# Group C's projections read the latents in row order through a strided moving operand

## The chip, the cores and the metric

The kernel runs on one core of a Trainium2 chip. The core has five engines that run side by side and wait for each other by semaphores: TensorE (PE, matmuls; its weight loads are a row of their own, PEld), VectorE (DVE), ScalarE (ACT), GpSimd (POOL) and SyncE (SP, which issues most transfers). The metric is the time of one execution in microseconds, the median of several runs. Beside the times there is one profiled execution, with every instruction's start and duration.

## The reference

Two layers of a mixer over 512 latent tokens (a grid of 8 rows by 64 columns) and 256 context tokens. Each layer normalises and modulates its input, projects it once, runs three groups of attention heads on parts of the projection, multiplies their outputs by a SiLU gate, projects back and adds. Group A is global attention, group B a neighbourhood on the grid, group C a sliding window over the tokens in row order. Only what concerns the change is shown.

```
def layer(x, cx, ..., need_ctx):
    hx = rmsnorm(x, norm_w) * (1 + scale[:, None, :]) + shift[:, None, :]
    hc = rmsnorm(cx, norm_w) * (1 + scale_c) + shift_c
    px = split_cols(hx @ w_in)
    pc = split_cols(hc @ w_in)
    ...
    yc_, ycc = window_gqa(px[6], px[7], px[8], pc[6], pc[7], pc[8], cos, sin, sink, need_ctx)
    ux = jnp.concatenate([ya, yb, yc_], axis=-1) * jax.nn.silu(px[9])
    x = x + gate[:, None, :] * (ux @ w_out)

def window_gqa(q, k, v, qc, kc, vc, cos, sin, sink, need_ctx):
    """+-WINDOW sliding-window GQA with per-head sink logit, banded 128-query blocks."""
    q = (apply_rope(heads(q, N_HEADS_C), cos, sin) * scale).reshape(B, N, N_KV_C, G, HEAD_DIM)
    k = apply_rope(heads(k, N_KV_C), cos, sin)
    ...
```

## The kernel before

**Layout.** The latents lie in SBUF with the model dimension on partitions, eight tiles of 128, and the tokens along the free dimension. The tokens stand in column order: position 8 * column + row, so that group B's window on the grid is a contiguous stretch of keys. Each tile exists twice, as a rounded high part (`hh`) and the remainder (`hl`), in the matmul type fp32r; weights are split in the same way (`wh`, `wl`). A product is the sum of three matmuls, high by high, high by low, low by high. The latents' tiles are called hL in the profile, the context's hC.

**Projections.** There are two kinds. `proj_t` has the latents as stationary operand and gives tokens on partitions; it serves group A, B's values and gates. `proj_f` has the weights as stationary operand and streams the tokens through as moving operand: 24 matmuls (8 tiles by 3 products) of 512 latent columns, and 24 of 256 context columns where the layer needs them, all accumulated in one bank of PSUM. It serves B's queries and keys and everything of group C: in each layer four pairs of query heads, one key, one value and four gates. The matmuls stand at L313 for both groups. `cols` gives the moving operand, a plain slice of the tile.

**Row order for group C.** C's window runs over tokens in row order, position 64 * row + column. Before the change the projection leaves the bank in column order, and the copy out of PSUM turns it: in `rope_c` (queries and keys, L968) and in `c_kv` (values, L1003) ACT reads the bank straight through and writes SBUF with a step of 64 elements. `rope_c` then issues four DMAs that swap halves of the head (tile tB), and POOL does the rotation (L974 to L976). The gate (`c_g`) is not turned: ACT's Tanh (L1020) and a DVE product (L1021) leave it in column order in the tile gc. At the end of a pair, `finish` scales the heads' output OT (row order), and POOL multiplies it by the gate (L1344): it reads OT with a step of 64 and the gate straight, and writes u in column order, as the output projection wants it.

**What sets the order.** A hand-written plan (`PLAN`) says which projections are made while which pair of heads attends; `weave` alternates between the two by estimated PE times, and Python's order of calls, with priorities for the copies out of PSUM, sets each engine's queue. Group C's key, value and first pair are made during A's first pair, and the other three C pairs during A's and C's pairs that follow. Attention's own steps are: scores into the bank Sbig, a row maximum on DVE, the exponential on ACT, transposes on PE into the bank T, copies out as high and low parts (ACT pth, DVE ptl), and the sums over values into Obig. Projections have two banks, named pj. At a layer's end the output projection (L514, `out_mm`) takes up C's last pair last; u is split for it by ACT and POOL or DVE (`split_u`, L486 and L487).

Of the kernel before, what the change touches and what calls it, by code (L numbers as in the profile page):

```python
# [14 lines left out]
AF = mybir.ActivationFunctionType  # L15
# [6 lines left out]
NT = 512  # L22
# [30 lines left out]
WF_BQ, WF_BK, WF_CQ, WF_CK, WF_CV, WF_CG = 0, 4, 8, 12, 13, 14  # L53
# [10 lines left out]
def body(tc, xT, small, bcast, rpb, adaw, adat, wt, wf, wo, trigA, trigC, mskB, mskC, outT):  # L64
    nc = tc.nc
# [33 lines left out]
    def after(inst, name):  # L99

        tc.add_manual_dep(inst.ins, name, mybir.DependencyInfo(mybir.DependencyClass.NoSync,
                                                               mybir.DependencyReason.DATA), reason="bank")
# [154 lines left out]
    def load_wf(l, s):  # L257
        return load_w(wf[l, s], (4, 128))
# [14 lines left out]
    def cols(h, c0, n):  # L273
        return h[0][:, c0:c0 + n] if c0 < NT else h[1][:, c0 - NT:c0 - NT + n]
# [16 lines left out]
    def paced(mm, i):  # L291

        if i % 3 == 0 and pace["at"]:
            after(mm, pace["at"])
# [2 lines left out]

        return h[2][:, t * 128:t * 128 + 128] if t < 4 else cols(h, t * 128, 128)

    def proj_f(l, s, need_ctx, bank, done):  # L300

        banks = early.pop(("f", s), None)
        w = None if banks else load_wf(l, s)
        for c0, n in ((0, NT), (NT, NCX)):
            if c0 and not need_ctx:
                continue
            p = banks.pop(0) if banks else bank()
            i = 0
            for kt in range(KT if w else 0):
                wh, wl = w[kt // 4]  # L310
                r = kt % 4
                for a, b in ((wh, hh), (wh, hl), (wl, hh)):
                    paced(nc.tensor.matmul(p[:, 0:n], a[:, r, :], cols(b[kt], c0, n), start=(i == 0),  # L313
                                           stop=(i == 23)), i)
                    i += 1
                yield 3 * n / 2400
            with tc.high_priority(offset=CFG["hpf"]):
                done(p[:, 0:n], c0, n)
# [60 lines left out]
    with tc.tile_pool(name="p0", bufs=1, reuse_waits="tile") as p0:  # L379
# [51 lines left out]
        for kt in range(KT):  # L431
# [19 lines left out]
            for t in (1, 2, 3, 4, 5, 0):  # L451
                p = early["t", WT_BV][t // 2][:, t % 2 * 256:t % 2 * 256 + 256]
# [84 lines left out]
    for l in range(2):  # L537
# [3 lines left out]
        with tc.tile_pool(name=f"p2_{l}", bufs=1, reuse_waits="tile") as p2:  # L541
# [147 lines left out]
            rows = []  # L689
# [64 lines left out]
            n = 0  # L754
# [12 lines left out]
def mixers(tc, nc, l, last, p1, ps, const, env):  # L767
# [8 lines left out]
    need_cq = not last  # L776

    def slot(name, dt=F32):
        tag = CFG["map"].get(name, name)
        return p1.tile([128, NA], dt, name=name, tag=tag, bufs=CFG[tag])  # L780
# [83 lines left out]
    def v_copy(V, src, t2):  # L864

        src = src.rearrange("p t (h f) -> p t h f", h=2)
        hi = V[:, t2:t2 + 2, :, 0, :]
        copy(hi, src, "cv")
        nc.vector.tensor_sub(V[:, t2:t2 + 2, :, 1, :], src, hi.bitcast(F32))
# [84 lines left out]
    def rowmajor(ap):  # L954
        return ap.rearrange("p (r c) -> p c r", r=8)

    def colmajor(ap):
        return ap.rearrange("p (c r) -> p c r", r=8)

    def rope_c(s, scale, need_ctx, bank):  # L960
        q = p1.tile([128, NT], F32, name="tA", bufs=CFG["tA"])
        r = slot("tR")

        def done(p, c0, n):
            if c0:
                nc.scalar.activation(r[:, NT:NA], p, AF.Copy, scale=scale)
            else:
                nc.scalar.activation(rowmajor(q), colmajor(p), AF.Copy, scale=scale)  # L968

        yield from proj_f(l, s, need_ctx, bank, done)  # L970
        sw = p1.tile([128, NT], F32, name="tB", bufs=CFG["tA"])
        for b in range(4):
            nc.scalar.dma_start(sw[b * 32:(b + 1) * 32], q[(b ^ 1) * 32:((b ^ 1) + 1) * 32])
        en("cr0").tensor_mul(r[:, 0:NT], q, tabs["C", 0])  # L974
        en("cr1").tensor_mul(sw, sw, tabs["C", 1])
        en("cr2").tensor_add(r[:, 0:NT], r[:, 0:NT], sw)  # L976
        return r
# [10 lines left out]
    def c_kv(bank):  # L988
        r = yield from rope_c(WF_CK, 1.0, True, bank)
        K = [newK() for _ in range(2)]  # L990
        for h in range(2):
            o, x = 64 * h, 64 * (1 - h)
            k = K[h]
            nc.scalar.activation(k[o:o + 64, 0], r[o:o + 64], AF.Copy)
            en("cklo").tensor_sub(k[o:o + 64, 1], r[o:o + 64], k[o:o + 64, 0].bitcast(F32))
            en("ckcp").tensor_copy(k[x:x + 64], k[o:o + 64].bitcast(F32))
        v = slot("tR")

        def done(p, c0, n):
            if c0:  # L1000
                nc.scalar.activation(v[:, NT:NA], p, AF.Copy)
            else:
                nc.scalar.activation(rowmajor(v[:, 0:NT]), colmajor(p), AF.Copy)  # L1003

        yield from proj_f(l, WF_CV, True, bank, done)
        V = newV()
        for t2 in range(0, 6, 2):
            T = psT()
            for t in range(2):
                nc.tensor.transpose(T[:, t * 128:(t + 1) * 128], v[:, (t2 + t) * 128:(t2 + t + 1) * 128], ident)  # L1010
            v_copy(V, T[:, 0:256].rearrange("p (t f) -> p t f", t=2), t2)
        return K, V

    def c_g(i, bank):

        G = p1.tile([128, NA], F32, name="gc", tag="bm", bufs=CFG["bm"])

        def done(p, c0, n):
            th = p1.tile([128, NT], F32, name="th", bufs=1)
            nc.scalar.activation(th[:, 0:n], p, AF.Tanh, scale=0.5)  # L1020
            nc.vector.scalar_tensor_tensor(G[:, c0:c0 + n], th[:, 0:n], 1.0, p, op0=OP.add, op1=OP.mult)  # L1021

        yield from proj_f(l, WF_CG + i, need_cq, bank, done)
        return G

    def c_pair(i, bank):
# [21 lines left out]
    def turn(*args, **kw):  # L1048
        m = nc.tensor.transpose(*args, **kw)  # L1049
        pace["pe"] = m.ins.name  # L1050
        return m
# [258 lines left out]
    def finish(c):  # L1310
        kind, i, G, OT, sums, negm = [c[k] for k in ("kind", "i", "G", "OT", "sums", "negm")]
        if callable(G):
            G = G()
        if kind == "C":
            ex = p1.tile([128, 12], F32, name="ex", bufs=2)
            for h in range(2):
                j = BC_SINK + l * 8 + 2 * i + h
                nc.scalar.activation(ex[:, h * 6:h * 6 + nq], negm[:, h * 6:h * 6 + nq], AF.Exp, bias=bc[:, j:j + 1])
                nc.vector.tensor_add(sums[:, h * 6:h * 6 + nq], sums[:, h * 6:h * 6 + nq], ex[:, h * 6:h * 6 + nq])
        rec = p1.tile([128, 2, 6], F32, name="rec", bufs=2)  # L1320
        nc.vector.reciprocal(rec[:, :, 0:nq], sums.rearrange("p (h t) -> p h t", h=2)[:, :, 0:nq])
        if kind == "C":
            R = slot("tR")
        else:
            R = G
        R = R.rearrange("p (t h f) -> p t h f", h=2, f=64)
        u = slot("u")
        ft = {"A": 0, "B": 4, "C": 8}[kind] + i
        for t in range(nq):
            src = onesw[:, None, :].to_broadcast([128, 2, 64]) if kind == "C" else R[:, t]  # L1330
            en("fin").tensor_mul(R[:, t], src, rec[:, :, t:t + 1].to_broadcast([128, 2, 64]))
        yield 0
        for c0, n in ((0, 4), (4, nq - 4)):
            if not n:
                continue
            T = psT()
            for t in range(n):
                turn(T[:, t * 128:(t + 1) * 128],
                                    R[:, c0 + t].rearrange("p h f -> p (h f)"), ident)
            a, b = c0 * 128, (c0 + n) * 128  # L1340
            if kind == "C":
                nc.vector.scalar_tensor_tensor(OT[:, a:b], OT[:, a:b], 0.5, T[:, 0:b - a], op0=OP.mult, op1=OP.mult)
                if c0 == 0:
                    nc.gpsimd.tensor_mul(colmajor(u[:, 0:NT]), rowmajor(OT[:, 0:NT]), colmajor(G[:, 0:NT]))  # L1344
                else:
                    nc.gpsimd.tensor_mul(u[:, a:b], OT[:, a:b], G[:, a:b])
            else:
                nc.vector.scalar_tensor_tensor(u[:, a:b], OT[:, a:b], 0.5, T[:, 0:b - a], op0=OP.mult, op1=OP.mult)
            yield n * 0.11
        if ft in FT_ORDER[-KEEP:]:  # L1350
            t = g_["new_u"](FT_ORDER.index(ft))
            g_["split_u"](t, u, ncol, 1)
            g_["ua"][0][ft], g_["ua"][1][ft] = t
        else:
            d = dram.tile([128, NA], F32, name=f"u{l}_{ft}")
            nc.scalar.dma_start(d[:, 0:ncol], u[:, 0:ncol])
            udram[l, ft] = d
# [163 lines left out]
    for pair, items, n_ada in PLAN:  # L1521
# [3 lines left out]
        if pair is not None:  # L1525
            kind, i = pair
# [3 lines left out]
            else:  # L1530
                Q, G = made[kind.lower(), i]
# [11 lines left out]
    Q, G = made["c", 3]  # L1543
# [115 lines left out]
```

## Time and profile before

| | us |
|---|---|
| timed runs, median of 3 (lowest, highest) | 1203.47 (1203.21, 1205.78) |
| the profiled execution's own time | 1204.83 |
| its span, first instruction to last | 1203.0 |

How to read it: the timed runs are the metric; the profiled execution is one run with the profiler on, and its own time is 1.8 us above its span, which lies around the first and last instruction. All durations below are from that one execution. A group of the profile is a set of instructions of one line, engine, operation and shape, with its names as out<-in; for matmuls out<-moving,stationary. Behind the count stand the busy time in us, the mean duration in ns, then the engine's idle time just before them and who ended it. Matmuls are pipelined, so the duration of one (several hundred ns) is longer than the spacing of their starts.

### The profile page before, as it was taken

The numbers are of one execution on the slowest core, as the hardware profiler recorded it, in microseconds if no ns is written. First come the engines' busy times: TensorE is split into PE (matmuls) and PEld (weight loads), VectorE is DVE, ScalarE is ACT, GpSimd is POOL, SyncE is SP. The second block draws the span as 40 slices with busy tenths as digits, with TensorE's granted clock in tenths as the row PEclk, the third lists the DMA queues.
The fourth block names the chain that finished last, engine by engine and source line by source line (L and its number), as shares of the span: only waits on it lengthen the run. The fifth ranks groups of instructions, "written<-read, shape, count | busy, mean of one in ns | idle before, by whom it ended". The sixth has DMA issues, their size and how long they took to land.

```text
span 1203.0 us, 21757 instructions
## 1 busy us (share of the span) xinstructions
PE 1157.8 (96%) x8016; PEld 1037.1 (86%) x8016; DVE 765.8 (64%) x1541; ACT 697.5 (58%) x1581; POOL 418.4 (35%) x511
## 2 busy tenths in 40 slices
PE   5999999999999999999999999999999999989997
PEld 3898999998898988988877998989988888878876
DVE  5666576764555666577568896667754556667553
ACT  5446555655656576588523543555666667677552
POOL 1441110234446354467110030202274564556001
PEclk9999999999999999999999999999999999999999
DMA  9552222323222112113176662323222111223152
GB/s 327 204 141 89 78 77 64 123 67 102 80 93 91 64 48 84 50 55 126 27 268 213 210 207 74 100 81 111 89 72 69 53 46 52 62 70 90 35 159 78
DMA packets 60826, 124.22 MB, mean 103 GB/s; under 512 B 7216, under 2 KB 13488, under 8 KB 60720
## 3 DMA queue, kind: packets, MB, share of 16 engines
q1 hardware_dynamic: 54768, 111.96, 29.0%
q10 hardware_dynamic: 5952, 10.88, 2.7%
q8 instruction: 63, 1.03, 0.3%
q14 instruction: 43, 0.35, 0.1%
HBM read 109.05 MB, written 11.14 MB: 100 GB/s over the span
## 4 chain that ended last, share of the span: by engine, by line
PE 83%; DVE 6%; ACT 4%; DMA 3%; issue 3%; POOL 1%; ACTq 0%; SPq 0%; DVEq 0%; POOLq 0%
PE pj L313 19%; PE pj L336 17%; PE Sbig L1044 10%; PE Obig L1044 9%; PE T L1049 9%; PE pj L514 4%; PE T L514 3%; PE Sbig L514 2%; PE T L336 2%; PE Sbig L425 1%; ACT pth L793 1%; PE pj L425 1%; DVE ptl L1039 1%; PE Sbig L336 1%; PE pj L209 1%
## 5 line engine op out<-in xcount | busy, mean ns | idle before, releaser
L1039 DVE TENSOR_TENSOR ptl<-T,pth 128x512 fp32r<-128x512 f32 (+2 forms) x312 | 181.0, 590 | 124.0 <-ACT pth L793 121.9
L793 ACT ACTIVATE pth<-T 128x512 fp32r<-128x512 f32 (+2 forms) x312 | 159.1, 520 | 136.2 <-PE T L1049 127.6
L336 PE MATMUL pj<-wh,hL 128*128 128x256 f32 x896 | 180.8, 287 | 0.1
L313 PE MATMUL pj<-hL,wh 128*128 128x512 f32 x544 | 175.2, 401 | 0.9 <-ACT wh L242 0.5
L242 ACT ACTIVATE wh<-ws 128x512 fp32r<-128x512 f32 x192 | 119.8, 629 | 88.1 <-PE pj L313 17.1
L1049 PE MATMUL T<-ident,P 128*128 128x128 f32 x1024 | 166.2, 273 | 3.9 <-ACT qt L897 2.2
L1044 PE MATMUL Sbig<-kt,qt 128*128 128x256 f32 (+1 forms) x864 | 155.9, 308 | 2.2 <-ACT P L1155 1.2
L245 POOL TENSOR_TENSOR wl<-ws,wh 128x512 fp32r<-128x512 f32 x76 | 98.8, 1303 | 156.0 <-ACT wh L242 156.0
L336 PEld LDWEIGHTS pj<-wh,hL 128*128 128x128 f32 x896 | 144.4, 190 | 1.9 <-issue 0.6
L1044 PE MATMUL Obig<-pth,vt 128*128 128x256 f32 (+2 forms) x432 | 134.3, 320 | 6.4 <-ACT pth L793 3.1
L1049 PEld LDWEIGHTS T<-ident,P 128*128 128x128 f32 x1024 | 123.3, 140 | 17.0 <-ACT qt L897 2.9
L1044 PE MATMUL Obig<-ptl,vt 128*128 128x256 f32 (+2 forms) x432 | 132.1, 320 | 4.0 <-DVE ptl L1039 3.5
L1044 PEld LDWEIGHTS Sbig<-kt,qt 128*128 128x128 f32 x864 | 123.7, 190 | 10.6 <-DVE negm L1203 2.1
L336 PE MATMUL pj<-wl,hL 128*128 128x256 f32 x448 | 127.9, 286 | 0.0
L245 DVE TENSOR_TENSOR wl<-ws,wh 128x512 fp32r<-128x512 f32 x116 | 84.2, 733 | 43.5 <-ACT wh L242 39.6
L313 PEld LDWEIGHTS pj<-hL,wh 128*128 128x128 f32 x544 | 96.1, 189 | 17.1 <-ACT wh L242 0.9
L313 PE MATMUL pj<-hL,wl 128*128 128x512 f32 x272 | 107.1, 394 | 0.2 <-DVE wl L245 0.2
L1044 PEld LDWEIGHTS Obig<-pth,vt 128*128 128x128 f32 x432 | 81.6, 189 | 18.1 <-ACT pth L793 9.6
L1044 PEld LDWEIGHTS Obig<-ptl,vt 128*128 128x128 f32 x432 | 81.6, 189 | 14.6 <-DVE ptl L1039 9.6
L1435 POOL TENSOR_TENSOR bm<-wr,bm 128x192 f32<-128x192 f32 (+1 forms) x48 | 40.6, 876 | 141.7 <-DMA bm<-mskB_dram 122.7
L1153 DVE TENSOR_REDUCE negm<-Sbig 128x1 f32<-128x768 f32 x64 | 61.1, 955 | 38.7 <-PE Sbig L1044 23.8
L336 PEld LDWEIGHTS pj<-wl,hL 128*128 128x128 f32 x448 | 85.4, 191 | 0.4
(334 smaller groups left out, 2508.6 us busy)
## 6 DMA issues: line engine op xcount, KB each, us to landing
ws<-wf_dram SPq DMA_DIRECT2D x72, 256.0 KB, 3.0
ws<-wt_dram SPq DMA_DIRECT2D x72, 256.0 KB, 3.0
ada<-adaw_dram SPq DMA_DIRECT2D x32, 512.0 KB, 5.3
ws<-wo_dram SPq DMA_DIRECT2D x57, 256.0 KB, 2.8
bm<-mskB_dram SPq DMA_DIRECT2D x16, 576.0 KB, 4.1
dw<-adat_dram SPq DMA_DIRECT2D x8, 512.0 KB, 7.4
dots<-adat_dram SPq DMA_DIRECT2D x16, 256.0 KB, 4.1
u<-u ACTq DMA_DIRECT2D x9, 384.0 KB, 3.1
```

Of the source, the lines that this page charges most:

```text
L242: nc.scalar.activation(hi, src, AF.Copy)
L245: eng.tensor_sub(lo, src, hi.bitcast(F32))
L313: paced(nc.tensor.matmul(p[:, 0:n], a[:, r, :], cols(b[kt], c0, n), start=(i == 0), stop=(i == 23)), i)
L336: paced(nc.tensor.matmul(p[:, t * 256:(t + 1) * 256], tok(a[kt], t2 + t), b[:, r, :], start=(i == 0), stop=(i == 23)), i)
L425: mm = nc.tensor.matmul(out, a, b, start=begin, stop=(kt == KT - 1 and i == 2), skip_group_check=True)
L514: mm = nc.tensor.matmul(p[:, 0:n], a[:, r, :], ucols(ua[b][ft], c0, n), start=(ft == FT_ORDER[0] and i == 0), stop=(ft == FT_ORDER[-1] and ...
L793: nc.scalar.activation(out, src, AF.Copy)
L1039: i = nc.vector.tensor_sub(lo[:, 0:n], T[:, 0:n], hi[:, 0:n].bitcast(F32))
L1044: m = nc.tensor.matmul(*args, **kw)
L1049: m = nc.tensor.transpose(*args, **kw)
L1153: nc.vector.tensor_reduce(nm, S, axis=AX.X, op=OP.max, negate=True)
L1435: nc.gpsimd.tensor_add(b, src, b)
```

## The change

The turn into row order moves from the copy out of PSUM to the matmul. `proj_f` gets a flag `rows`; where it is set, the latents' moving operand is read as 8 runs of 64 elements with a step of 8 elements (`rowwise`), and the bank fills in row order. Only the calls of group C set it. The copies of queries, keys and values out of PSUM become plain. The gate now comes in row order too, so POOL's product at the end of a pair reads it with a step of 64, as it does OT.

```diff
+    def rowwise(ap):
+
+        return ap.rearrange("p (c r) -> p r c", r=8)
+
-    def proj_f(l, s, need_ctx, bank, done):
+    def proj_f(l, s, need_ctx, bank, done, rows=False):
...
                 for a, b in ((wh, hh), (wh, hl), (wl, hh)):
-                    paced(nc.tensor.matmul(p[:, 0:n], a[:, r, :], cols(b[kt], c0, n), start=(i == 0),
-                                           stop=(i == 23)), i)
+                    out, x = p[:, 0:n], cols(b[kt], c0, n)
+                    if rows and c0 == 0:
+                        out, x = out.rearrange("p (r c) -> p r c", r=8), rowwise(x)
+                    paced(nc.tensor.matmul(out, a[:, r, :], x, start=(i == 0), stop=(i == 23)), i)
...
             if c0:
                 nc.scalar.activation(r[:, NT:NA], p, AF.Copy, scale=scale)
             else:
-                nc.scalar.activation(rowmajor(q), colmajor(p), AF.Copy, scale=scale)
+                nc.scalar.activation(q, p, AF.Copy, scale=scale)
-        yield from proj_f(l, s, need_ctx, bank, done)
+        yield from proj_f(l, s, need_ctx, bank, done, True)
...
-                nc.scalar.activation(rowmajor(v[:, 0:NT]), colmajor(p), AF.Copy)
+                nc.scalar.activation(v[:, 0:NT], p, AF.Copy)
-        yield from proj_f(l, WF_CV, True, bank, done)
+        yield from proj_f(l, WF_CV, True, bank, done, True)
...
-        yield from proj_f(l, WF_CG + i, need_cq, bank, done)
+        yield from proj_f(l, WF_CG + i, need_cq, bank, done, True)
...
-                    nc.gpsimd.tensor_mul(colmajor(u[:, 0:NT]), rowmajor(OT[:, 0:NT]), colmajor(G[:, 0:NT]))
+                    nc.gpsimd.tensor_mul(colmajor(u[:, 0:NT]), rowmajor(OT[:, 0:NT]), rowmajor(G[:, 0:NT]))
```

The new lines shift the numbers: L313 becomes L320, and lines from `rope_c` on stand six higher. Each engine's instructions are as many as before, and nearly all stand in the same order. On ACT, in layer 0, where the first C projection (the key) leaves its bank, the rows before the change are these (out<-in and the shape of what is written; tA is the copy, tB the halves swapped by DMA, qt group A's queries):

```order
L889 ACTIVATE qd<-tC 128x4x64
L968 ACTIVATE tA<-pj 128x64x8
L973 DMA tB<-tA 32x512
L897 ACTIVATE qt<-T 128x256 x2
L973 DMA tB<-tA 32x512
```

and after it:

```order
L895 ACTIVATE qd<-tC 128x4x64
L974 ACTIVATE tA<-pj 128x512
L979 DMA tB<-tA 32x512
L903 ACTIVATE qt<-T 128x256 x2
L979 DMA tB<-tA 32x512
```

Nothing moved there; the copy alone has another shape, 512 elements in one run instead of 64 by 8. On PE, the matmuls of that first projection stand like this after the change, between attention's matmuls (L1050 and L1055), exactly as they stood before it at L313, L1044 and L1049; the stepped operand doesn't show in the row, since the shape is that of what is written:

```order
L320 MATMUL pj<-hL,wl 128x512
L1050 MATMUL Obig<-ptl,vt 128x512
L1055 MATMUL T<-ident,P 128x128 x2
L320 MATMUL pj<-hL,wh 128x512 x2
L320 MATMUL pj<-hL,wl 128x512
L320 MATMUL pj<-hL,wh 128x512 x2
L320 MATMUL pj<-hL,wl 128x512
```

Here, too, nothing moved. The few rows that did move stand elsewhere: one matmul of the context passes a neighbour in layer 0's output projection, and a handful of rows on DVE, ACT and SP around it change places by one or two.

## The prediction

> **What bounds the kernel now.** I read the page first: its span, the busy time, and the chain that ended last.
>
> ```profile
> span 1203.0 us, 21757 instructions
> ...
> PE 1157.8 (96%) x8016; PEld 1037.1 (86%) x8016; DVE 765.8 (64%) x1541; ACT 697.5 (58%) x1581; POOL 418.4 (35%) x511
> ...
> PE 83%; DVE 6%; ACT 4%; DMA 3%; issue 3%; POOL 1%; ACTq 0%; SPq 0%; DVEq 0%; POOLq 0%
> PE pj L313 19%; PE pj L336 17%; PE Sbig L1044 10%; PE Obig L1044 9%; PE T L1049 9%; PE pj L514 4%; PE T L514 3%; PE Sbig L514 2%; PE T L336 2%; PE Sbig L425 1%; ACT pth L793 1%; PE pj L425 1%; DVE ptl L1039 1%; PE Sbig L336 1%; PE pj L209 1%
> ```
>
> The reader is to see that TensorE (PE) is the bound: it holds 83% of the chain, and its largest single share is L313, the very matmuls whose moving operand the change makes strided. ACT, which the change relieves, holds 4%.
>
> An average hides stages, so next come the busy times of the six stretches in which group C's projections are made (three of layer 0, three of layer 1; the first columns are the stretch, its length, PE busy and count).
>
> ```profile
> 262.00:365.00 103.00, 102.93 (x742) 89.91 (x741) 55.93 (x119) 61.13 (x143) 51.12 (x55) 1.00 0.28 92
> 365.00:470.00 105.00, 102.58 (x739) 91.21 (x738) 64.68 (x125) 67.67 (x159) 56.91 (x69) 0.98 0.24 76
> 470.00:565.00 95.00, 92.39 (x674) 83.94 (x673) 63.56 (x119) 69.34 (x163) 50.75 (x58) 1.00 0.20 64
> 873.00:960.00 87.00, 83.49 (x553) 74.38 (x551) 47.03 (x90) 55.10 (x121) 50.28 (x52) 1.00 0.21 67
> 960.00:1042.00 82.00, 79.86 (x539) 71.57 (x540) 48.29 (x88) 56.83 (x125) 44.39 (x50) 1.00 0.15 49
> 1042.00:1102.00 60.00, 55.85 (x366) 49.04 (x364) 38.54 (x70) 44.90 (x100) 34.64 (x40) 1.00 0.28 84
> sum 532.00, PE 517.12 PEld 460.04 DVE 318.04 ACT 354.96 POOL 288.08; mean PE 86.19 PEld 76.67 DVE 53.01 ACT 59.16 POOL 48.01
> ```
>
> In these 532 us PE is idle for only 532.00 - 517.12 = 14.9 us, at a granted clock of 0.98 to 1.00. ACT is busy for 67% and POOL for 54%. So time added to PE here has at most 14.9 us of idle time to vanish in, and time taken from ACT has nearly nothing to shorten.
>
> **How many matmuls change.** The groups of L313 by form, first between 262 and 565 us, then between 873 and 1102 us (names are out<-moving,stationary):
>
> ```profile
> L313 PE MATMUL pj<-hL,wh 128*128 128x512 f32 x160 | 52.4, 405 | 0.0
> ...
> L313 PE MATMUL pj<-hL,wl 128*128 128x512 f32 x80 | 31.6, 395 | 0.0
> ...
> L313 PE MATMUL pj<-hL,wh 128*128 128x512 f32 x160 | 51.4, 402 | 0.0
> L313 PE MATMUL pj<-hL,wl 128*128 128x512 f32 x80 | 31.5, 393 | 0.0
> ```
>
> That is 160 + 80 in each layer, 480 in all, which the code confirms: ten projections a layer (four query pairs, key, value, four gates) of 24 matmuls each. The context's matmuls (128x256, from hC) stay plain, and so do group B's. No instruction is added or removed; the order on every engine is practically that of before.
>
> **What such a matmul costs now.** Minimum, median and maximum in ns of L313's two forms, and a few rows of the timeline (start, duration):
>
> ```profile
> L313 PE MATMUL pj<-hL,wh x544: 387/393/500, 87.1 to 1097.8; 128*128 128x512 f32 x182
> L313 PE MATMUL pj<-hC,wh x336: 274/283/562, 93.1 to 902.0; 128*128 128x256 f32 x168
> ```
>
> ```profile
> 276.13 0.63 PE L313 MATMUL pj<-hL,wh 128*128 128x512 f32 x2
> 276.60 0.39 PE L313 MATMUL pj<-hL,wl 128*128 128x512 f32 x1
> 276.83 0.63 PE L313 MATMUL pj<-hL,wh 128*128 128x512 f32 x2
> ```
>
> 256 more columns take 393 - 283 = 110 ns, so 0.43 ns for each column, and 512 columns stream for 220 ns. The timeline agrees: three matmuls start within 276.83 - 276.13 = 0.70 us, 0.233 us apart, so streaming is nearly the whole of the spacing.
>
> **The price of the strided read is the one unknown that matters.** After the change the 512 columns are read as 8 runs of 64 elements, each element 8 floats (32 bytes) from the one before. No matmul in this trace reads its moving operand so. I bound it by the two places where another engine steps through SBUF. ACT's copies out of PSUM (L968, L1003) write with a step of 64 floats; L1020 reads the same kind of bank and writes plainly:
>
> ```profile
> L968 ACT ACTIVATE tA<-pj 128x512 f32<-128x512 f32 x10 | 10.9, 1094 | 1.0 <-PE pj L313 0.9
> L1020 ACT ACTIVATE th<-pj 128x512 f32<-128x512 f32 x8 | 4.7, 588 | 0.0
> L1003 ACT ACTIVATE tR<-pj 128x512 f32<-128x512 f32 x2 | 2.2, 1110 | 0.5 <-POOL gt L1331 0.3
> L1020 ACT ACTIVATE th<-pj 128x256 f32<-128x256 f32 x4 | 1.5, 378 | 0.0
> ```
>
> Plainly ACT takes (588 - 378)/256 = 0.82 ns an element after a fixed 168 ns; with the step (1094 - 168)/512 = 1.81 ns, 2.2 times as much. POOL's gate product (L1344) reads one of two operands with that step; L976 reads both plainly:
>
> ```profile
> L976 POOL TENSOR_TENSOR tR<-tR,tB 128x512 f32<-128x512 f32 x10 | 12.9, 1290 | 0.3
> L1344 POOL TENSOR_TENSOR u<-OT,gc 128x512 f32<-128x512 f32 x8 | 12.6, 1569 | 26.4 <-DVE OT L1342 26.4
> L825 POOL TENSOR_TENSOR tC<-qs,tab 128x256 f32<-128x256 f32 x15 | 11.2, 750 | 34.8 <-ACT qs L816 34.6
> ```
>
> Plainly POOL takes (1290 - 750)/256 = 2.11 ns an element; the step adds (1569 - 1290)/512 = 0.54 ns, a factor of 1.26. So from below, the price on PE is nothing (PE may fetch far enough ahead); a gain is excluded, since the same 512 columns pass through the array. By POOL's factor it is 0.26 x 220 = 57 ns a matmul, 27 us over 480. By ACT's factor it is 1.2 x 220 = 264 ns, 127 us. By POOL's 0.54 ns added to each element it is 276 ns, 133 us. If a lone element took ACT's 1.81 ns outright, it would be (1.81 - 0.43) x 512 = 707 ns, 339 us.
>
> I take a factor of **2**: nearest to ACT's, because ACT is the engine nearest in pace (0.82 ns an element against PE's 0.43, where POOL's 2.11 ns leaves room in which most of an extra access hides), and because two neighbours on PE take 0.86 ns, about what ACT needs for one, which is what one access for each element instead of one for two would give. That makes 220 ns x 480 = **+105.6 us** on PE.
>
> [...]
>
> **What of it is hidden.** In C's stages attention's matmuls are woven between the projections, and PE waits now and then for ACT or DVE; a longer projection matmul ahead of such a wait gives the other engine more time. Of the 14.9 us of idle time I take 10 as filled (bounds 0 and 14.9): some waits stand where no projection is left ahead of them. So PE adds 95.6 us.
>
> **The copies.** Twelve copies fall from about 1.1 to 0.59 us, 12 x 0.51 = 6.1 us of ACT. The waits on the tile tA say what this is worth (engine and line, us in total, times):
>
> ```profile
>   POOL tR L974: 6.1, 2
> ...
>   PEld pj L336: 0.2, 1
> ```
>
> PE waited 0.2 us for it. POOL's waits for L968 feed rotated queries of a pair that attention takes up only a stage later. I count -0.2 us; what is late next is PE itself.
>
> **The gate in row order.** The Tanh and the product on DVE (L1020, L1021) only see their columns in another order. The last product on POOL (L1344) now steps through two operands instead of one: by the row above 0.28 us more, at most twice that, 8 x 0.28 = 2.2 us of POOL in all. It could show at a layer's end, where the output projection waits for C's last pair:
>
> ```profile
> 1149.72 1.56 POOL L1344 TENSOR_TENSOR u<-OT,gc 128x512 f32<-128x512 f32 x1 [12.57 <-DVE OT L1342]
> 1152.02 1.29 POOL L487 TENSOR_TENSOR hL<-u,hL 128x512 fp32r<-128x512 f32 x1 [0.74 <-ACT hL L486]
> ```
>
> ```profile
> 1155.64 0.61 PE L514 MATMUL pj<-hL,wh 128*128 128x512 f32 x2
> ```
>
> The split of it ends at 1152.02 + 1.29 = 1153.31, and PE takes its matmul up at 1155.64: 2.3 us of cover, under which I cost the 0.28 us at nothing. Were the cover gone, it would be 0.3 us a layer.
>
> **The sum.** The profiled execution took 1204.83 us (its span is 1203.0, and 1.8 lie around it): 1204.83 + 105.6 - 10 - 0.2 = 1300.2. The median of the three timed runs, 1203.47, is 1.4 below the profiled one, so I predict **1299 us**. This case's own range goes from all idle time filled with a somewhat smaller factor, 1285, to POOL's 133 us with nothing hidden, 1204.8 + 133 - 1.4, about 1336.
>
> **The rivals.**
> - **PE reads it at full pace.** If the moving operand is fetched ahead with enough ports, or its price is under 14.9 us/480 = 31 ns a matmul (0.06 ns a column) so that idle time swallows it, the change is not slower. Then ACT's 6.1 us and POOL's 2.2 us decide: between -2 us (L968 and L1003 are 13.1 of ACT's 697.5 us, so about 2% of its 4% of the chain, 0.9 us; doubled, as a bound) and +0.5 us. That is 1203 us, 1201 to 1204. For it: PE's stream is regular and long; against it: both stepped rows of this trace pay. [...]
> - **A part price.** POOL's factor of 1.26 gives 27 us, less 5 of idle time: 1204.8 + 22 - 1.4, about 1225. For it: POOL's is the only stepped read; against: POOL is five times slower an element than PE, so it hides most.
> - **A lone element has its own fixed time.** ACT's 1.81 ns outright gives 339 us, less 15: about 1527. For it: ACT's number as it stands; against: it was a write, with another step.
>
> **How the numbers follow.** Factor 2 and its neighbours (1285 to 1336): 0.52. Full pace: 0.26. Part price (1206 to 1285): 0.11. Fixed time (above 1336): 0.11. The range runs from full pace to the end of factor 2, 1201 to 1336, and leaves out the last case and the edges. A measurement of this kernel tells apart about 0.2% (2.4 us). Of the full pace 0.08 is faster by more, 0.17 within, 0.01 slower; with the other three, slower has 0.75.
>
> **What would show it.** Right: starts of three latent matmuls of a C projection about 1.36 us apart instead of 0.70, the 512-column form at a median near 610 ns, the C stages longer by some 95 us together with less idle time on PE, group B's L313 matmuls unchanged at 393 ns, the copies at 0.59 us, the gate product at 1.85 us. Wrong: C's triples still 0.70 us apart (full pace), or 2.8 us apart (fixed time); or the clock granted to PE falling in these stages, which no term holds.

## The result and the profile after

| | before | after |
|---|---|---|
| timed runs, median of 5 (lowest, highest), us | 1203.52 (1203.21, 1205.78) | 1296.58 (1293.34, 1300.1) |
| span of the profiled execution, us | 1203.0 | 1294.8 |

The change makes the kernel slower by a ratio of 1.0761, with a 95% interval of 1.0744 to 1.0777, or 93 us. The forecast was 1299 us.

The page of the kernel after, its span, busy times and the chain that ended last:

```profile
span 1294.8 us, 21757 instructions
...
PE 1250.8 (97%) x8016; PEld 1045.8 (81%) x8016; DVE 763.7 (59%) x1541; ACT 693.2 (54%) x1581; POOL 423.3 (33%) x511
...
PE 87%; DVE 4%; ACT 3%; DMA 3%; issue 2%; SPq 0%; POOL 0%; DVEq 0%; ACTq 0%
PE pj L320 25%; PE pj L342 16%; PE Sbig L1050 9%; PE Obig L1050 9%; PE T L1055 8%; PE pj L520 4%; PE T L520 3%; PE Sbig L520 2%; PE T L342 2%; PE Sbig L431 1%; DMA ws<-wo_dram 1%; PE pj L431 1%; PE Sbig L342 1%; ACT pth L799 1%; DVE ptl L1045 1%
```

The counts are the same. The chain's share of the projection line, L313 before and L320 now, went from 19% to 25%: 0.25 x 1294.8 - 0.19 x 1203.0 = 95 us by these rounded shares, the whole loss. PE's busy time rose by 93 us, ACT's fell by 4, POOL's rose by 5.

Both traces hold the same 8016 matmuls, practically in the same order, so the n-th of one can be set beside the n-th of the other. How much later it starts says where the time came in:

| the matmul that started before at | starts after at | later by, us | what lies between it and the row above |
|---|---|---|---|
| 262.03 | 261.93 | -0.1 | all that comes ahead of C's projections of layer 0 |
| 565.03 | 610.73 | 45.7 | C's projections of layer 0 |
| 873.01 | 918.73 | 45.7 | end of layer 0, group B of layer 1 |
| 1102.70 | 1193.57 | 90.9 | C's projections of layer 1 |
| 1195.98 | 1287.72 | 91.7 | the end |

All but 1 us of it comes in while C's projections run, half in each layer. The same six stretches as before, with their borders moved along (stretch, length, then busy time and count of PE, PEld, DVE, ACT, POOL, then the granted clock):

```profile
262.00:388.00 126.00, 125.93 (x742) 92.22 (x742) 56.45 (x122) 61.62 (x146) 53.72 (x60) 1.00 0.24 78
388.00:505.00 117.00, 114.87 (x734) 90.43 (x733) 61.54 (x124) 65.59 (x153) 55.08 (x64) 1.00 0.20 65
505.00:611.00 106.00, 103.48 (x678) 85.33 (x677) 63.52 (x117) 70.12 (x163) 51.47 (x58) 1.00 0.20 58
919.00:1028.00 109.00, 106.09 (x552) 76.50 (x550) 47.23 (x91) 53.63 (x122) 50.13 (x53) 1.00 0.17 52
1028.00:1125.00 97.00, 95.05 (x538) 73.95 (x538) 48.15 (x87) 55.72 (x124) 45.83 (x50) 0.98 0.13 42
1125.00:1194.00 69.00, 65.78 (x369) 50.35 (x368) 40.38 (x71) 45.99 (x101) 37.35 (x41) 1.00 0.25 73
sum 624.00, PE 611.22 PEld 468.79 DVE 317.28 ACT 352.67 POOL 293.58; mean PE 101.87 PEld 78.13 DVE 52.88 ACT 58.78 POOL 48.93
```

They last 624 us instead of 532. PE is idle in them for 624.00 - 611.22 = 12.8 us, where it was 14.9. The granted clock stands at 0.98 to 1.00, so the clock has no part in it.

The timeline shows the matmuls themselves, at the same place as in the prediction (start, duration):

```profile
280.85 1.02 PE L320 MATMUL pj<-hL,wh 128*128 128x512 f32 x2
281.69 0.61 PE L320 MATMUL pj<-hL,wl 128*128 128x512 f32 x1
282.12 1.04 PE L320 MATMUL pj<-hL,wh 128*128 128x512 f32 x2
```

Three starts take 282.12 - 280.85 = 1.27 us where they took 0.70. Over all 480 stepped matmuls of the trace, the median from one's start to the next matmul's is 431 ns, and was 231; the means are 436 and 240. Group B's 336 latent matmuls of the same line, read plainly, have a median of 228 ns before and 227 after. The other parts of the change, by groups of ACT and of POOL:

```profile
L974 ACT ACTIVATE tA<-pj 128x512 f32<-128x512 f32 x10 | 5.9, 590 | 6.2 <-PE pj L320 6.2
...
L1009 ACT ACTIVATE tR<-pj 128x512 f32<-128x512 f32 x2 | 1.2, 598 | 1.6 <-PE pj L320 1.6
```

```profile
L1350 POOL TENSOR_TENSOR u<-OT,gc 128x512 f32<-128x512 f32 x8 | 17.7, 2208 | 26.4 <-DVE OT L1348 26.4
```

The copies became 0.5 us shorter each, as foreseen, and ACT now sits idle ahead of them until PE is done. POOL's gate product went from 1.57 to 2.21 us, more than foreseen.

### The profile page after: what moved, and what is told of

Same layout as the page of the kernel before. It is cut to its first block, busy times and chain, and to the rows that moved or that the text cites. A ratio compares the mean times of both kernels' runs of the same rounds, so it can differ in the third digit from the quotient of the medians.

```text
span 1294.8 us, 21757 instructions
## 1 busy us (share of the span) xinstructions
PE 1250.8 (97%) x8016; PEld 1045.8 (81%) x8016; DVE 763.7 (59%) x1541; ACT 693.2 (54%) x1581; POOL 423.3 (33%) x511
## 4 chain that ended last, share of the span: by engine, by line
PE 87%; DVE 4%; ACT 3%; DMA 3%; issue 2%; SPq 0%; POOL 0%; DVEq 0%; ACTq 0%
PE pj L320 25%; PE pj L342 16%; PE Sbig L1050 9%; PE Obig L1050 9%; PE T L1055 8%; PE pj L520 4%; PE T L520 3%; PE Sbig L520 2%; PE T L342 2%; PE Sbig L431 1%; DMA ws<-wo_dram 1%; PE pj L431 1%; PE Sbig L342 1%; ACT pth L799 1%; DVE ptl L1045 1%
## 5 line engine op out<-in xcount | busy, mean ns | idle before, releaser
L320 PE MATMUL pj<-hL,wh 128*128 128x512 f32 x544 | 240.9, 528 | 0.9 <-ACT wh L242 0.5
L1055 PE MATMUL T<-ident,P 128*128 128x128 f32 x1024 | 166.5, 274 | 3.8 <-ACT qt L903 2.2
L245 POOL TENSOR_TENSOR wl<-ws,wh 128x512 fp32r<-128x512 f32 x76 | 98.8, 1303 | 208.9 <-ACT wh L242 208.0
L1050 PE MATMUL Sbig<-kt,qt 128*128 128x256 f32 (+1 forms) x864 | 156.3, 308 | 2.1 <-ACT P L1161 1.1
L320 PE MATMUL pj<-hL,wl 128*128 128x512 f32 x272 | 142.4, 523 | 0.4 <-DVE wl L245 0.4
L1055 PEld LDWEIGHTS T<-ident,P 128*128 128x128 f32 x1024 | 123.9, 141 | 22.2 <-issue 7.5
L1050 PE MATMUL Obig<-pth,vt 128*128 128x256 f32 (+2 forms) x432 | 135.0, 322 | 6.3 <-ACT pth L799 3.2
L320 PEld LDWEIGHTS pj<-hL,wh 128*128 128x128 f32 x544 | 99.3, 195 | 49.2 <-issue 40.1
L1050 PEld LDWEIGHTS Sbig<-kt,qt 128*128 128x128 f32 x864 | 124.5, 191 | 15.7 <-issue 7.2
L1050 PE MATMUL Obig<-ptl,vt 128*128 128x256 f32 (+2 forms) x432 | 131.7, 319 | 3.6 <-DVE ptl L1045 3.4
L245 DVE TENSOR_TENSOR wl<-ws,wh 128x512 fp32r<-128x512 f32 x116 | 85.0, 740 | 45.1 <-ACT wh L242 40.9
L1050 PEld LDWEIGHTS Obig<-pth,vt 128*128 128x128 f32 x432 | 82.3, 191 | 23.3 <-ACT pth L799 10.1
L1050 PEld LDWEIGHTS Obig<-ptl,vt 128*128 128x128 f32 x432 | 82.0, 190 | 16.5 <-DVE ptl L1045 8.2
```

Of the source, the lines that this page charges most:

```text
L245: eng.tensor_sub(lo, src, hi.bitcast(F32))
L320: paced(nc.tensor.matmul(out, a[:, r, :], x, start=(i == 0), stop=(i == 23)), i)
L1050: m = nc.tensor.matmul(*args, **kw)
```

## The experiments

Two questions were open. Is the stepped read the whole loss, or do the copies and the gate have a part? And what about the pattern makes PE read at half pace: the distance between elements, the number of runs and dimensions, or the addresses at which they lie? A single number, 431 ns, answers neither. In all edits below, `-` is the changed kernel unless said otherwise, and the theories go by the letters that the expectations give them. The first two experiments were timed several times; of the others there is one run each, which differences of 100 us and the spacings in the traces allow.

**The change without its strided operand.**

```diff
-                    if rows and c0 == 0:
+                    if False:
```

> The change without its strided operand: C's matmuls read the latents plainly again, but the twelve copies stay plain and POOL's gate product stays with two stepped operands (the tokens reach group C in column order, so the output isn't the reference's). If the whole loss is the stepped read: 1202 to 1206 us, not to be told from before beyond what POOL's slower product costs; the prediction's term for the copies is -0.2 us and for POOL 0. If the copies were worth more than their waits showed: below 1201 us. If POOL's product, now 2.2 us instead of 1.57, stands on the path: above 1206 us.

Measured: 1205.5 us (12 runs) against 1206.12 (17) on the same chip, a ratio of 0.9992 (0.9979 to 1.0006). No effect to be told from none, though POOL's product took 2.09 us in it:

```profile
L1350 POOL TENSOR_TENSOR u<-OT,gc 128x512 f32<-128x512 f32 x8 | 16.7, 2093 | 26.4 <-DVE OT L1348 26.4
```

So the plain copies and the slower product together don't show in the time; within this interval the stepped matmuls are the whole loss. It also speaks against a gain from any cheaper way of getting row order: with plain reads in place of stepped ones, plain copies and all, nothing that could be measured was won.

**The gates' projections plain, the rest of the change kept.** The output stays the reference's.

```diff
-        yield from proj_f(l, WF_CG + i, need_cq, bank, done, True)
+        yield from proj_f(l, WF_CG + i, need_cq, bank, done)
...
-                    nc.gpsimd.tensor_mul(colmajor(u[:, 0:NT]), rowmajor(OT[:, 0:NT]), rowmajor(G[:, 0:NT]))
+                    nc.gpsimd.tensor_mul(colmajor(u[:, 0:NT]), rowmajor(OT[:, 0:NT]), colmajor(G[:, 0:NT]))
```

> The change with the gates' projections as before: the 192 matmuls of the eight gates read plainly, the gate stays in column order and POOL's product is that of before; queries, keys and values (288 matmuls) keep the stepped read. If the loss goes by the count of stepped matmuls, 288/480 of the 93 us stays: 1203.5 + 56 = 1259 us (1252 to 1266 with idle time filled differently). If POOL's product or the gate's stage made a good part of it: clearly below 1250 us.

Measured: 1259.17 us (4 runs), ratio 1.044 (1.0418 to 1.0462). 288 stepped matmuls of 480 should leave three fifths of the 7.6%, 4.6%, which lies inside the interval; so the loss goes by the count.

**The step: every second, fourth, sixteenth float.** Only the pattern changes, with `out` split into as many runs; for every second float:

```diff
-        return ap.rearrange("p (c r) -> p r c", r=8)
+        return ap.rearrange("p (c r) -> p r c", r=2)
```

> The changed kernel, but the 480 stepped matmuls read every second float (2 runs of 256 elements, step 8 bytes) instead of every eighth. The tokens come in another order, so the output isn't the reference's; everything else stays. Theory A (PE gets 16-byte pieces of SBUF and keeps pace as long as two elements come from each): 0.23 us between starts, about 1203 us. Theory B (it gets pairs of neighbouring floats, 8 bytes, and every element that is not the neighbour of the one before needs a fetch of its own): 0.43 us, about 1297 us. Theory C (the price comes with the number of runs and dimensions of the pattern, not with the step): near 0.23 us, about 1203 us, since there are 2 runs instead of 8.

> As above with every fourth float (4 runs of 128 elements, step 16 bytes; the output isn't the reference's). Theory A: one element from each 16-byte piece, so 0.43 us between starts and about 1297 us, as with step 8. Theory B: the same, 0.43 us and 1297 us. Theory C: about half of the price of 8 runs, 0.33 us, about 1250 us.

> As above with every sixteenth float (16 runs of 32 elements, step 64 bytes; the output isn't the reference's). Theories A and B: one fetch for each element however far apart, 0.43 us between starts, about 1297 us. Theory C: twice the price of 8 runs, 0.63 us, about 1390 us. Theory D (elements a power of two apart fall into the same bank of SBUF, the more the larger the step): above 0.43 us, above 1310 us.

Measured, beside 1205.09 us of the kernel before on the same chip: 1309.1, 1309.47 and 1297.89 us. The rows of the timeline are those of step 2, then of step 4, then of step 16:

```profile
281.01 1.07 PE L320 MATMUL pj<-hL,wh 128*128 128x512 f32 x2
281.89 0.63 PE L320 MATMUL pj<-hL,wl 128*128 128x512 f32 x1
282.35 1.08 PE L320 MATMUL pj<-hL,wh 128*128 128x512 f32 x2
```

```profile
279.74 1.08 PE L320 MATMUL pj<-hL,wh 128*128 128x512 f32 x2
280.64 0.64 PE L320 MATMUL pj<-hL,wl 128*128 128x512 f32 x1
281.11 1.11 PE L320 MATMUL pj<-hL,wh 128*128 128x512 f32 x2
```

```profile
279.31 1.03 PE L320 MATMUL pj<-hL,wh 128*128 128x512 f32 x2
280.16 0.62 PE L320 MATMUL pj<-hL,wl 128*128 128x512 f32 x1
280.60 1.05 PE L320 MATMUL pj<-hL,wh 128*128 128x512 f32 x2
```

Three starts take 1.34, 1.37 and 1.29 us; the median spacings are 452, 461 and 434 ns. Theory A falls, since two floats from each 16-byte piece (step 2) don't keep the pace: 452 ns, against 231 before the change. Theory C falls, since 2 runs cost as much as 16. Theory D falls, since the longest step is not the dearest.

**Pairs of neighbours.** Two neighbouring floats at a time, 64 bytes from one pair to the next, as far as the single floats of step 16.

```diff
-        return ap.rearrange("p (c r) -> p r c", r=8)
+        return ap.rearrange("p (c r e) -> p r c e", r=8, e=2)
```

> As above, but pairs of neighbouring floats are read with a step of 16 floats (64 bytes) between pairs: 8 runs of 32 pairs, a pattern of three dimensions (the output isn't the reference's). Theory A and theory B: two elements from each piece, so full pace, 0.23 us between starts and about 1203 us. Theory C (runs and dimensions): at least the price of the change, 0.43 us or more, 1297 us or more.

Measured: 1300.9 us. The timeline:

```profile
280.81 1.03 PE L320 MATMUL pj<-hL,wh 128*128 128x512 f32 x2
281.66 0.61 PE L320 MATMUL pj<-hL,wl 128*128 128x512 f32 x1
282.09 1.04 PE L320 MATMUL pj<-hL,wh 128*128 128x512 f32 x2
```

1.28 us for three, a median of 431 ns. Theory B falls too: pairs of neighbours cost what single elements do. What was left was that any pattern but a single run is read at half pace (theory E), or that more than two neighbours are needed (theory G).

**Runs of 256, 64 and 4 neighbours.** For runs of 4:

```diff
-        return ap.rearrange("p (c r) -> p r c", r=8)
+        return ap.rearrange("p (a b c) -> p b a c", b=2, c=4)
```

> The changed kernel, but the 480 matmuls read two plain runs of 256 neighbouring floats with a gap of 32 floats between them (the output isn't the reference's). Theory E (any moving operand that is not one single run is read at half pace): 0.43 us between starts, about 1297 us. Theory G (full pace as long as more than two neighbours follow each other): 0.23 us, about 1203 us. Theory H (each break between neighbours has its price; the pairs' 256 breaks cost 0.20 us, 0.78 ns a break): one break, 0.23 us, about 1203 us.

> As above with eight runs of 64 neighbouring floats, every second run first (the output isn't the reference's). Theory E: 0.43 us and 1297 us. Theory G: 0.23 us and 1203 us. Theory H: 8 breaks, 6 ns a matmul, about 1206 us.

> As above with 128 runs of 4 neighbouring floats (16 bytes each, on 16-byte borders), every second run first (the output isn't the reference's). Theory E: 0.43 us and 1297 us. Theory G: 0.23 us and 1203 us. Theory H: 128 breaks, 0.10 us a matmul, 0.33 us between starts, about 1250 us.

Measured, beside 1203.86 us on that chip: 1205.19, 1205.64 and 1207.02 us. The timeline of runs of 4:

```profile
284.33 0.63 PE L320 MATMUL pj<-hL,wh 128*128 128x512 f32 x2
284.79 0.40 PE L320 MATMUL pj<-hL,wl 128*128 128x512 f32 x1
285.02 0.63 PE L320 MATMUL pj<-hL,wh 128*128 128x512 f32 x2
```

0.69 us for three, a median of 233 ns: full pace with 128 runs in a pattern of three dimensions. Theory E falls, and so does H, which wanted 0.33 us; G is left. Between 2 and 4 neighbours lies the whole price; 3 were not tried.

**The same runs of 4, and one plain run, 8 bytes past a 16-byte border.** `b[kt][2]` is the tile from its first column, in which the latents start at column 64; column 62 is 248 bytes on, 8 past a border if the tile begins on one, which the runs of 4 at full pace (233 ns) bear out.

```diff
-                        out, x = out.rearrange("p (b a c) -> p b a c", b=2, c=4), rowwise(x)
+                        out, x = out.rearrange("p (b a c) -> p b a c", b=2, c=4), rowwise(b[kt][2][:, 62:574])
```

> The kernel with 128 runs of 4 neighbouring floats, but starting 8 bytes past a 16-byte border, so that each run lies in two 16-byte pieces (the output isn't the reference's). If PE gets whole 16-byte pieces by address: half pace or between, 0.33 to 0.43 us between starts, 1250 to 1297 us. If what counts is only that the pattern's innermost run is four elements long: 0.233 us, 1203 to 1207 us.

```diff
-                        out, x = out.rearrange("p (r c) -> p r c", r=8), rowwise(x)
+                        x = b[kt][2][:, 62:574]
```

> The changed kernel, but the 480 matmuls read one plain run of 512 floats that starts 8 bytes past a 16-byte border (two tokens are shifted in, so the output isn't the reference's). Theory M (a mode: full pace only where every group of four successive columns is one 16-byte piece on its border, otherwise one column in 0.84 ns): 0.43 us between starts, about 1297 to 1310 us. Theory N (the count of pieces that are begun: a long run has one piece more than an aligned one, wherever it starts): 0.23 us, 1203 to 1207 us.

Measured: 1310.02 us for the runs of 4 and 1204.54 us for the plain run, where the kernel before took 1206.12 and 1208.57 on these chips. Their timelines, in this order:

```profile
281.01 1.07 PE L320 MATMUL pj<-hL,wh 128*128 128x512 f32 x2
281.89 0.64 PE L320 MATMUL pj<-hL,wl 128*128 128x512 f32 x1
282.35 1.09 PE L320 MATMUL pj<-hL,wh 128*128 128x512 f32 x2
```

```profile
284.51 0.63 PE L320 MATMUL pj<-hL,wh 128*128 128x512 f32 x2
284.97 0.39 PE L320 MATMUL pj<-hL,wl 128*128 128x512 f32 x1
285.21 0.63 PE L320 MATMUL pj<-hL,wh 128*128 128x512 f32 x2
```

1.34 us against 0.70; medians 453 and 232 ns. The first is a little slower than the 1297 us expected at most, and has the spacing of step 2. Runs of four neighbours lost the pace (453 ns) when each lay across a 16-byte border, although the shape of the pattern is the same and only the address differs, by 8 bytes. So in these runs the addresses decided: 233 ns where each 16-byte run lay in one 16-byte piece, 453 where it lay in two; theory G, by the length of the runs alone, doesn't suffice. The long run that starts off a border lost nothing (232 ns), so theory M falls: the borders crossed within it cost nothing that shows. Theory N, the count of pieces begun, fits these two: 128 or 129 pieces for 512 columns went at full pace (233 and 232 ns), 256 at half (453).

It doesn't fit everything: single elements with a step of 4, 8 or 16 begin 512 pieces, and went at half pace (461, 431 and 434 ns) as pairs did (256 pieces, 431 ns), not at a quarter. So the runs show two levels: as good as all pieces used whole, by columns that follow each other, or not. Why there is no third level, and why steps 2 and 4 take 20 to 30 ns more than steps 8 and 16, stays open.

**The step on the weights instead.** Here `-` is the kernel before.

```diff
-        tok = tok or (lambda h, t: cols(h, t * 128, 128))
+        tok = tok or (lambda h, t: h[0].rearrange("p (c r) -> p r c", r=4)[:, t] if t < 4 else cols(h, t * 128, 128))
```

> The kernel before, but in the projections of group A, and in group B's gates, the latents as stationary operand are read with a step of 4 floats (the moving operand, the weights, stays plain; the tokens come in another order, so the output isn't the reference's). If a stepped read is slow for weight loads as it is for the moving operand, a load goes from 190 ns to 300 ns or more, longer than the 120 ns between starts of these 128x256 matmuls can hide, and these several hundred pairs become 0.1 us longer each: 1270 us or more. If the price belongs to the moving operand alone: 1203 to 1207 us, loads at 190 ns.

Measured: 1350.36 us beside 1203.86. Loads of stepped latents (hL) against those of the context, which stay plain (hC); minimum, median and maximum in ns:

```profile
L336 PEld LDWEIGHTS pj<-wl,hL x448: 187/329/335, 125.9 to 1212.4; 128*128 128x128 f32 x150
...
L336 PEld LDWEIGHTS pj<-wl,hC x160: 187/192/193, 91.3 to 962.0; 128*128 128x128 f32 x160
```

The first row's median is a stepped load; 64 loads of group B's values stay plain in it, hence its minimum. A load takes 329 instead of 192 ns, 1.1 ns more for each of its 128 columns. So here the stationary operand paid for the step as the moving one did. In all rows of the line together 1344 loads are stepped, and with their matmuls, of 256 columns each, the median from one start to the next goes from 120 to 233 ns: 1344 x 0.113 = 152 us, where the kernel loses 147. Shorter steps, pairs and borders were not tried on this operand.

## Why the prediction was right

- **The bound.** PE was read as the bound with 14.9 us of idle time in C's stages. That held: almost all that PE gained in length is in the time.
- **The count.** 480 matmuls, confirmed by the stages in the table and by the gates' run, whose 288 gave three fifths of the loss.
- **The price.** The forecast took a factor of 2 on the streaming time, +220 ns; measured +200 ns by the medians and +196 ns by the means. That a stepped matmul streams at about half pace was right, and the size 10% too large: 480 x 0.196 = 94 us instead of 105.6. The forecast laid its 220 ns on top of the whole spacing of 0.233 us, a factor of 1.94 on the spacing; from 231 to 431 ns it was 1.87. Why it stays under 2 is open.
- **The reason for the factor** was only half right. The forecast had it that two neighbours share an access and a lone element needs its own. That was the author's estimate; no trace shows accesses. The runs say otherwise: two floats of a 16-byte piece did not suffice, neither as a pair of neighbours (431 ns) nor as every second float (452 ns), while four on a 16-byte border did (233 ns). So the factor was chosen among bounds from 57 to 707 ns by its nearness to ACT's 2.2 and by a reason that the runs bear out only in part, and that it came so near is in part luck.
- **What was hidden.** 10 us of idle time were to be filled. PE's idle time in the stages went from 14.9 to 12.8 us, so about 2 were. This error and that of the price nearly cancel: 105.6 - 10 = 95.6 forecast, 94 - 2 = 92 measured (the spans differ by 91.8). The forecast's nearness to the result owes something to that.
- **The copies.** 1.1 to 0.59 us, 6 us of ACT, worth nothing that can be measured, as forecast; the run without the step gives 0.9992 with 1 inside its interval.
- **POOL's product.** Forecast at 1.85 us and 2.12 at most, measured 2.21 as the mean of eight that took 2.06 to 2.54; 2.09 in the run without the stepped matmuls. So the second stepped operand cost 0.52 to 0.64 us, about twice the first's 0.28. The forecast put it at nothing in the time, under 2.3 us of cover at the end of layer 1, and the same cover stands there after the change. These are the last part of u's split on POOL and the matmul that takes it up on PE:

```profile
1243.76 1.29 POOL L493 TENSOR_TENSOR hL<-u,hL 128x512 fp32r<-128x512 f32 x1 [0.74 <-ACT hL L492]
```

```profile
1247.38 0.62 PE L520 MATMUL pj<-hL,wh 128*128 128x512 f32 x2
```

  The split ends at 1243.76 + 1.29 = 1245.05 and PE takes it up at 1247.38. But a wait of PE a few us earlier, which the forecast did not look at, did grow. It is for DVE's split of a weight (L245). Before the change:

```profile
1150.74 1.09 DVE L245 TENSOR_TENSOR wl<-ws,wh 128x512 fp32r<-128x512 f32 x1 [1.16 <-ACT wh L242]
1151.88 0.50 PE L514 MATMUL T<-hL,wl 128*128 128x512 f32 x1 [0.39 <-DVE wl L245]
```

  and after it:

```profile
1240.96 2.06 POOL L1350 TENSOR_TENSOR u<-OT,gc 128x512 f32<-128x512 f32 x1 [12.56 <-DVE OT L1348]
1241.97 1.60 DVE L245 TENSOR_TENSOR wl<-ws,wh 128x512 fp32r<-128x512 f32 x1 [1.15 <-ACT wh L242]
1243.62 0.50 PE L520 MATMUL T<-hL,wl 128*128 128x512 f32 x1 [0.91 <-DVE wl L245]
```

  Such a split on DVE takes 0.69 us in the median; beside POOL's product it took 1.09, and beside the longer product 1.60, ending 0.55 us after POOL each time. PE's wait grew from 0.39 to 0.91 us. The runs agree that it is the product: with the product plain again (the gates' run) the split takes 1.11 us and PE waits 0.42; without the stepped matmuls, but with the product at 2.06, they are 1.60 and 0.90. So the term was 0.5 us and not nothing, too little to tell in the times.
- **The rivals.** Full pace would have needed a price under 31 ns a matmul; it was 200. The part price (57 ns) and the fixed time of 1.81 ns a column (707 ns) are both out, by the starts 1.27 us apart. By the spacing of the starts a column took 0.45 ns (231/512) in plain operands and 0.84 (431/512) in stepped ones, at a granted clock of 0.98 to 1.00 both times.

## What to carry to other kernels

The permutation put into the matmuls' access pattern wasn't free here: it cost 93 us, about 0.2 us for each of 480 matmuls. With the 4-byte elements of this kernel, a moving operand kept its pace in runs of four neighbours that fill 16-byte pieces (233 ns for 512 columns), or in one long run, on a border (231) or 8 bytes past one (232); single elements, pairs, and runs of four across the borders went at about half pace (431 to 461 ns). Runs of other lengths off the borders were not tried. A stationary operand read with a step of 16 bytes took 1.7 times as long to load (329 ns against 192). Where PE is the bound, leave the turn to a copy on an engine that has slack, even if it nearly doubles that copy, as here (1.1 us against 0.59). When the price of an operation isn't in the trace, take its bounds from what other engines pay for the same pattern, and multiply by the count before looking at what is saved.

## What the runs showed of the hardware that was not expected

- The price of a broken-up moving operand had two levels only: 231 to 233 ns for 512 columns in whole pieces or in one long run, 431 to 461 ns for everything else that was tried, whether two floats of a piece are used or one, and whether the step is 8 or 64 bytes.
- A long run that starts 8 bytes off a 16-byte border cost nothing (232 ns), while runs of four that do took as long as single elements (453 ns).
- A second stepped operand cost POOL's product more than the first: 1.29 us with none (L976, the rotation), 1.57 with one, 2.09 to 2.21 with two.
- Beside a longer product on POOL, an operation that DVE ran at the same time took longer: DVE's split of a weight took 0.69 us in the median, 1.09 beside the product of 1.56 us and 1.60 beside that of 2.06.
